# One pool of eight PSUM banks for a hybrid attention layer, scores visited by free banks, two value products joined, and a new order

## The chip, the cores and the metric

The kernel runs on one core of one Trainium2 chip. The time is device microseconds (us) of one execution of the program, and the figure compared is the median of several runs. A profile is one execution taken by the hardware profiler; its span is the time from the first to the last instruction, and the execution's own time is a little longer. TensorE (PE) does matrix products and transposes and writes them to PSUM, which has eight banks of 128 partitions × 512 float32. VectorE (DVE) and ScalarE (ACT) read PSUM and work in SBUF, GpSimd (POOL) works in SBUF, SyncE (SP) issues nearly all transfers (DMAs).

## The reference, cut

One decoder layer, sequence 2048, width 1024, all in float32. A projection makes 4096 columns from the normalised input; 12 heads of 64 attend with three dilated windows, mixed by their softmax denominators; the rest is a gated short convolution; then an output projection, a norm, and the residual.

```python
h = rmsnorm(x, norm_pre_g)
z = jnp.einsum('bsd,de->bse', h, w_in)
q, k, v, g_attn, c_h, c_b, c_c, g_conv = jnp.split(z, cuts, axis=-1)
q = rope(q.reshape(B, S, N_ATTN_HEADS, HEAD_DIM), pos)
k = rope(k.reshape(B, S, N_ATTN_HEADS, HEAD_DIM), pos)
for window, dilation in ((128, 1), (512, 4), (2048, 16)):
    o_i, lse_i = dilated_window_attn(q, k, v, window, dilation)
mix_w = jax.nn.softmax(jnp.stack(lses, axis=0), axis=0)
o = jnp.sum(mix_w[..., None] * jnp.stack(outs, axis=0), axis=0)
attn_out = o.reshape(B, S, ATTN_WIDTH) * jax.nn.silu(g_attn)
conv_out = c_b * causal_depthwise_conv(c_c * c_h, conv_w) * jax.nn.silu(g_conv)
y = jnp.einsum('bse,ed->bsd', jnp.concatenate([attn_out, conv_out], -1), w_out)
x = x + rmsnorm(y, norm_post_g)
```

## The kernel before

The work is cut into 32 units: eight groups of 512 projected columns (group 0 and 7 are the convolution's, 1 to 6 hold one pair of heads each), and for each group four blocks b = 0 to 3 of 512 positions. There are thus 24 attention units. A float32 product is made of three products of fp32r parts (high × high, high × low, low × high), which is why most things come in threes.

**A unit's projection** (from L917): four banks z, each the sum of 8 × 3 matmuls 128x512 (L936 to L938). In an attention unit two banks are made at a time (keys and queries, then values and gate), so a pair of banks takes 48 matmuls; in a convolution unit all four are made together.

**A unit's attention** (attn_unit): ACT and DVE take q and k out of PSUM, rotate them and split them; POOL makes a copy of q in another order for the nearest window (Q1, L646). Then PE makes scores. score4 (L686, matmuls in L694) makes them for the two wider windows, score1 (L711, L722) for the nearest one. Each uses the 64 rows of one head, and the two heads of the pair run side by side on the two halves of the array's rows, into two banks, one per head. A call makes one group: score4 handles 4, 2, 1, 1 of the four residues at b = 0, 1, 2, 3, and score1 two of four blocks, so that a unit has 3, 4, 6, 6 groups. DVE then takes the scores out of PSUM with mask and row minimum (L701, L729), ACT makes exponentials (L705, L733). parts (L740) transposes the probabilities, on PE (L762) with ACT and DVE splitting the result (L767, L768), or on DVE for far blocks (L753 to L755). times (L773) multiplies value tiles with the transposed probabilities: matmuls of 256 columns (L784), the columns being 128 queries, high and low part, into one of two banks O per head. gather (L790) takes O out (L800 to L802).

**The end**: the output projection in seven products per 256 × 1024 block (L1104 to L1106), its norm and the residual.

**What sets the order.** Nothing above is issued at once. Every step is an operation in a plan (add, L166) with an engine, an estimated duration, a priority and the tiles that it reads and writes. schedule (L199) walks through time and gives each engine, whenever it is free, the ready operation of the lowest priority number for which all tiles can be had (_take, L276). Tiles come from rings of slots; a PSUM bank is a slot. The operations are then written out in the order of their planned start, and each engine's queue and the DMA queue are run in that order on the chip. The mode of a PE operation (0 full matmul, 1 scores, 2 transpose) adds to its planned duration when it changes; in modes 1 and 2 the planner first looks for an operation that is also of mode 1 or 2. shift (L190) adds to priorities what the table SHIFT (L117) has for a pair of unit number and place in the code; the table holds what a search found.

PSUM before is parted in two rings: z with 3 banks in a fixed order for projections (L362), st with 5 for all else (L363); convolution units may use 3 + 1 (L364); the output projection uses all eight (L1047). Scores are put into the plan two groups at a time, as one PE operation that needs all four banks:

```python
for i in range(0, len(groups), 2):
    visit = groups[i:i + 2]
    score_last.append(add("PE", sum(g[0] for g in visit), pr, lambda visit=visit: [g[1]() for g in visit], ...
```

Of the kernel before, what the change touches and what calls it, by code (L numbers as in the profile page):

```python
# [28 lines left out]
F32 = mybir.dt.float32  # L29
# [5 lines left out]
DRAM = bass.MemoryType.DRAM  # L35

S, D, C = 2048, 1024, 512
KT = D // 128
NB = S // C
HD = 64  # L40
# [37 lines left out]
class Slot:  # L78
    __slots__ = ("ap", "free")
# [16 lines left out]
class Tok:  # L96


    __slots__ = ("ring", "slot", "left", "end", "hist", "n")
# [9 lines left out]


class Op:
    __slots__ = ("eng", "dur", "prio", "fn", "deps", "toks", "start", "end", "land", "wait", "outs", "ready", "n", "mode", "port", "data")

SHIFT = {  # L117
# [5 lines left out]
}  # L123


class Plan:
# [72 lines left out]
    def schedule(self):  # L199
        engines = ["PE", "ACT", "DVE", "POOL", "DMA"]  # L200
        free = dict.fromkeys(engines, 0.0)
        mode = dict.fromkeys(engines, 0)
        port = bytes_ = 0.0
        cand = {e: [] for e in engines}
        for o in self.ops:
            if not o.wait:
                heapq.heappush(cand[o.eng], (o.prio, o.n, o))
        events = [0.0]
        done = 0
        t = -1.0  # L210
        while done < len(self.ops):
            if not events:
                stuck = sorted((o.prio, o.n, o.eng) for e in engines for _, _, o in cand[e])[:20]
                raise RuntimeError(f"no progress at {t}: {stuck}")
            t2 = heapq.heappop(events)
            if t2 <= t:
                continue
            t = t2
            again = True
            while again:  # L220
                again = False
                for e in engines:
                    if free[e] > t:
                        continue
                    pick = None

                    for kept in ((True, False) if mode[e] else (False,)):
                        skipped = []
                        while cand[e]:
                            item = heapq.heappop(cand[e])  # L230
                            o = item[2]

                            if o.ready <= t and (o.mode or not kept) and not (o.port and port > t) \
                                    and not (o.data and bytes_ > t + 0.5) and self._take(o, t):
                                pick = o
                                break
                            skipped.append(item)
                        for item in skipped:
                            heapq.heappush(cand[e], item)
                        if pick is not None:  # L240
                            break
                    if pick is None:
                        continue
                    o = pick

                    if (o.mode == 1) != (mode[e] == 1):
                        o.dur += 0.2
                    if o.mode == 2 != mode[e]:
                        o.dur += 0.06
                    mode[e] = o.mode  # L250
                    o.start, o.end = t, t + max(o.dur, o.land)
                    if o.data:
                        bytes_ = max(bytes_, t) + o.data
                        o.end = max(o.end, bytes_ + 1.9)
                        heapq.heappush(events, bytes_ - 0.5)
                    free[e] = t + o.dur
                    if o.port:
                        port = free[e]
                    done += 1
                    again = True  # L260
                    heapq.heappush(events, free[e])
                    for k in o.toks:
                        k.left -= 1
                        k.end = max(k.end, o.end + self.lag(e, k.ring.eng))
                        if not k.left:
                            k.slot.free = k.end
                            heapq.heappush(events, k.end)
                    for q in o.outs:
                        q.ready = max(q.ready, o.end + self.lag(e, q.eng))
                        q.wait -= 1  # L270
                        if not q.wait:
                            heapq.heappush(cand[q.eng], (q.prio, q.n, q))
                            heapq.heappush(events, q.ready)
        return t

    def _take(self, op, t):  # L276

# [27 lines left out]


def mmt(n):
    return max(0.109, n * 0.000433 + 0.0071)


def actt(n, psum=False, ptr=False):
# [19 lines left out]
def hybrid_layer(ctx: ExitStack, tc: tile.TileContext, x, w_in, w_out, conv_w, g_pre, g_post,  # L331
                 rope, consts, out):
    nc = tc.nc
    mm = nc.tensor.matmul
# [3 lines left out]
    add = pl.add  # L338
# [4 lines left out]
    cp = ctx.enter_context(tc.tile_pool(name="const", bufs=1))  # L343
    dram = ctx.enter_context(tc.tile_pool(name="dram", bufs=1, space=DRAM))
    psum = ctx.enter_context(tc.tile_pool(name="psum", bufs=1, space=PSUM))

    def ring(pool_, name, n, shape, dt=F32, eng="ACT"):
        return Ring([Slot(pool_.tile(shape, dt, name=f"{name}{i}")) for i in range(n)], name != "st",
                    "PE" if pool_ is psum else eng)

    cst = cp.tile([128, 8 * 128], F32, name="cst")
    ident, perm, mask1, mask4 = cst[:, 0:128], cst[:, 128:256], cst[:, 256:512], cst[:, 512:1024]
    gp = cp.tile([128, KT], F32, name="gp")
    cw = cp.tile([128, 2, 3], F32, name="cw")
    t_d = [dram.tile([128, 3, C], F32, name=f"t{b}") for b in range(NB)]
    xt_d = [[dram.tile([128, 2, C], F32, name=f"xt{b}_{k}") for k in range(KT)] for b in range(NB)]
    mix_d = [dram.tile([KT, 128, C], F32, name=f"mix{b}") for b in range(NB)]
# [1 line left out]
    e_d = [dram.tile([4, 128, 4], F32, name=f"ed{i}") for i in range(2)]  # L359
    a_d = [dram.tile([32, 4, 4, 32], F32, name=f"ad{i}") for i in range(2)]  # L360

    z_r = ring(psum, "z", 3, [128, C])  # L362
    st_r = ring(psum, "st", 5, [128, C])  # L363
    zc_r = Ring(list(z_r) + list(st_r)[:1], False, "PE")  # L364

    xp_r = ring(cp, "xt", 9, [128, 2, C], F32R, "STREAM")
    wp_r = ring(cp, "w", 8, [128, 2, C], F32R)
# [221 lines left out]
    V1, V2 = {}, {}  # L589
    first_attn = []  # L590

    def attn_unit(n, p, b, zs):
# [147 lines left out]
        def parts(h, kind, blk, far=False):  # L740
# [16 lines left out]
            else:  # L757
                ps = Tok(st_r)

                def tr():  # L760
                    for i, (a, c) in enumerate(blk):
                        nc.tensor.transpose(ps.ap[:, i * 128:(i + 1) * 128], pp.ap[:, a, c * 128:(c + 1) * 128], ident)  # L762
                add("PE", 0.111 * m, pr, tr, r=[(pp, a) for a in tiles] + ["cst"], w=[ps, (pt, "hold")], mode=2)

                def p4():
                    return ps.ap[:, :m * 128].rearrange("p (i c) -> p i c", c=128)
# [4 lines left out]


        def times(h, kind, where, O):  # L773
            def pv():
                for (a, c), (pt, i) in sorted(where.items()):
                    dst = O.ap.rearrange("p (l q) -> p l q", l=2)[:, :, (a % 2) * 128:(a % 2 + 1) * 128]
                    if kind == 4:
                        v = V2[p * NB + c].ap[:, a].rearrange("p k d -> p (k d)")[:, h * 128:(h + 1) * 128]
                        s, e = c == 0, c == b
                    else:  # L780
                        t = 4 * b + a - 1 + c
                        v = V1[p * NB + t // 4].ap[:, t % 4, h * 128:(h + 1) * 128]
                        s, e = c == 0 or t == 0, c == 1
                    mm(dst, v, pt.ap[:, i], start=s, stop=e)  # L784
            vs = [V2[p * NB + c] for c in range(b + 1)] if kind == 4 else [V1[p * NB + c] for c in range(max(b - 1, 0), b + 1)]
            attn_last.append(add("PE", mmt(256) * len(where), pr, pv,
                                 r=[(pt, l) for pt in {pt for pt, _ in where.values()} for l in range(2)] + vs, w=[O]))

        UU = {}
# [16 lines left out]
            P[h, 4], P[h, 1] = Tok(p4_r), Tok(p1_r)  # L806

        groups = [score4(r) for r in range(0, 4, per)] + [score1(g) for g in (0, 2)]
        for i in range(0, len(groups), 2):
            visit = groups[i:i + 2]  # L810
            score_last.append(add("PE", sum(g[0] for g in visit), pr, lambda visit=visit: [g[1]() for g in visit], r=[k for g in visit for k in g[2]],
                w=[k for g in visit for k in g[3]], after=x_last, mode=1))
            for g in visit:
                g[4]()

        for kind in (4, 1):
            for h in range(2):
# [97 lines left out]
    for n in range(8 * NB):  # L915
# [12 lines left out]
        for pair in ((range(4),) if conv else (range(2), range(2, 4))):  # L928
          for kt in range(KT):
            for j in pair:  # L930
              xt, w = XT[n, kt], W[grp, kt] if conv else W[grp, j // 2, kt // 2]

              def proj(j=j, kt=kt, xt=xt, w=w, z=zs[j], conv=conv):
# [2 lines left out]
                mm(z.ap, w.ap[:, 0, js], xt.ap[:, 0], start=kt == 0, stop=False)  # L936
                mm(z.ap, w.ap[:, 0, js], xt.ap[:, 1], start=False, stop=False)  # L937
                mm(z.ap, w.ap[:, 1, js], xt.ap[:, 0], start=False, stop=kt == KT - 1)  # L938
              done = add("PE", 3 * (mmt(C) + 0.003), n * 100 + 50 + (kt if conv else j // 2 * 4 + kt / 2), proj, r=[xt, w], w=[zs[j]])
              if n == 0 and kt < 2:  # L940

                later = x_last[2 * kt + 2]
# [101 lines left out]
    tables = [Slot(cs_r[0].ap[:, i]) for i in range(3)]  # L1044
    gated(tables, [o for o in pl.ops if T_last in o.toks], lambda: None)
    xr_r = Ring(tables + list(raw_r))
    oz_r = Ring(list(z_r) + list(st_r), False, "PE")  # L1047
    for q in range(2 * NB):
        b, h = divmod(q, 2)
        po = 3400 + 100 * q  # L1050
# [160 lines left out]
```

## Time and profile before

| what | value |
|---|---|
| median of 3 runs | 1189.88 us (1188.49 to 1190.63) |
| profiled execution | 1189.55 us, its span 1187.8 us |
| score matmuls | L694 and L722, 576 each |
| value products, L784 | 852, mean 284 ns of one, 124.6 us busy |
| transposes of probabilities, L762 | 708, mean 273 ns of one, 98.6 us busy |
| stretch with attention on PE | 139 to 980 us |
| output projection on PE | 1028 to 1181 us |

The mean of one matmul is its time from start to end, and matmuls overlap in the array: a 128x512 row has 0.39 us, while the next starts 0.23 us after it. What PE spends on something is read from differences of starts in the timeline, not from the busy column.

### The profile page before, as it was taken

To read this page: it belongs to the slowest core of one execution; us is meant where nothing else is said; L and a number is where in the kernel's file an instruction comes from. 1 tells how busy PE (TensorE), PEld (TensorE's weight loads), DVE (VectorE), ACT (ScalarE), POOL (GpSimd) and SP (SyncE) were. 2 spreads that over 40 slices of the span, in tenths; PEclk is the share of its full clock that TensorE was granted. 3 is DMA by queue.
4 is the path that set the end of the run, shared out by engine and by line. 5 is a ranking of instruction groups with operands and counts; after the bars stand their busy time and mean duration, and the time that the engine had idled before them with its cause. 6 is when DMAs were issued, how large, how long until landed. Compare 5 with 4: busy or idle time off the path is not lost.

```text
span 1187.8 us, 20832 instructions
## 1 busy us (share of the span) xinstructions
PE 1175.5 (99%) x6716; PEld 981.5 (83%) x6716; DVE 924.7 (78%) x2331; ACT 715.1 (60%) x1875; POOL 266.7 (22%) x212
## 2 busy tenths in 40 slices
PE   9999999999999999999999999999999999999997
PEld 7788888888888888888888888888888888888886
DVE  4665568887788967897688977788788889888886
ACT  6433356765767776775567776576767554454443
POOL 0011123214223232213332222333322122200000
PEclk9999999999999999999999999999999999999999
DMA  9989767877678867687678777788757988645452
GB/s 339 366 340 349 258 227 234 249 246 211 191 212 262 276 198 215 181 289 238 236 229 224 249 201 220 231 262 258 214 162 248 324 260 296 210 145 182 138 186 89
DMA packets 175294, 280.46 MB, mean 236 GB/s; under 512 B 53712, under 2 KB 109776, under 8 KB 175184
## 3 DMA queue, kind: packets, MB, share of 16 engines
q1 hardware_dynamic: 174896, 278.86, 72.6%
q8 instruction: 53, 0.87, 0.3%
q14 instruction: 57, 0.47, 0.1%
q10 hardware_dynamic: 288, 0.27, 0.1%
HBM read 215.42 MB, written 51.05 MB: 224 GB/s over the span
## 4 chain that ended last, share of the span: by engine, by line
PE 92%; DMA 2%; DVE 2%; ACT 2%; issue 1%; SPq 0%; DVEq 0%; ACTq 0%
PE z L936 18%; PE z L938 17%; PE z L937 17%; PE st L784 8%; PE st L762 6%; PE st L694 4%; PE st L722 3%; PE st L1106 3%; PE st L1104 3%; PE st L1105 3%; PE z L1106 2%; PE z L1104 2%; PE z L1105 2%; PE st L936 1%; PE st L938 1%; PE st L937 1%
## 5 line engine op out<-in xcount | busy, mean ns | idle before, releaser
L936 PE MATMUL z<-xt,w 128*128 128x512 f32 x960 | 392.1, 408 | 0.7 <-DVE rp L561 0.5
L938 PE MATMUL z<-xt,w 128*128 128x512 f32 x960 | 375.6, 391 | 0.0
L937 PE MATMUL z<-xt,w 128*128 128x512 f32 x960 | 375.3, 391 | 0.0
L938 PEld LDWEIGHTS z<-xt,w 128*128 128x128 f32 x960 | 180.2, 188 | 39.7
L936 PEld LDWEIGHTS z<-xt,w 128*128 128x128 f32 x960 | 180.7, 188 | 39.1 <-issue 7.9
L937 PEld LDWEIGHTS z<-xt,w 128*128 128x128 f32 x960 | 181.1, 189 | 28.8 <-DVE xt L496 0.3
L705 ACT ACTIVATE p<-p,sm 128x128 f32<-128x128 f32 (+3 forms) x192 | 105.7, 553 | 59.0 <-DVE sm L701 58.9
L768 DVE TENSOR_TENSOR pt<-st,pt 128x512 fp32r<-128x512 f32 (+1 forms) x180 | 116.9, 675 | 24.9 <-ACT pt L767 23.4
L784 PEld LDWEIGHTS st<-pt,v 128*128 128x128 f32 x852 | 117.8, 190 | 12.5 <-DVE pt L768 2.0
L784 PE MATMUL st<-pt,v 128*128 128x256 f32 x852 | 124.6, 284 | 1.1 <-DVE pt L768 1.1
L802 DVE TENSOR_TENSOR uu<-st,uu 64x256 f32<-64x256 f32 x192 | 79.3, 420 | 58.0 <-ACT uu L801 50.4
L767 ACT CAST pt<-st 128x512 fp32r<-128x512 f32 (+1 forms) x180 | 98.3, 579 | 21.5 <-PE st L762 20.4
L800 ACT COPY uu<-st 64x256 f32<-64x256 f32 x192 | 69.5, 367 | 69.1 <-PE st L784 58.2
L701 DVE CUSTOM_DVE_ANT_0 p<-st,cst 128x128 f32<-128x128 f32 (+3 forms) x192 | 81.7, 486 | 31.0 <-PE st L694 30.6
L733 ACT ACTIVATE p<-p,e 128x256 f32<-128x256 f32 (+1 forms) x192 | 94.6, 496 | 18.4 <-DVE e L729 18.3
L844 POOL TENSOR_TENSOR uu<-uu 128x512 f32<-128x512 f32 x48 | 67.7, 1411 | 162.0 <-DVE uu L802 131.5
L762 PE MATMUL st<-cst,p 128*128 128x128 f32 x708 | 98.6, 273 | 0.0
L762 PEld LDWEIGHTS st<-cst,p 128*128 128x128 f32 x708 | 82.4, 141 | 12.5 <-issue 1.0
L801 ACT COPY uu<-st 64x256 f32<-64x256 f32 x192 | 68.8, 367 | 12.1 <-PE st L784 4.7
L729 DVE CUSTOM_DVE_ANT_0 p<-st,cst 128x256 f32<-128x256 f32 (+1 forms) x192 | 67.1, 410 | 9.4 <-PE st L722 9.3
L895 POOL TENSOR_TENSOR uu<-uu 128x512 f32<-128x512 f32 x24 | 36.6, 1527 | 164.9 <-DVE uu L894 164.9
L626 POOL TENSOR_TENSOR rp<-rp,cs 128x512 f32<-128x512 f32 x24 | 35.5, 1480 | 167.9 <-DMA rp<-rp 77.2
(287 smaller groups left out, 1934.1 us busy)
## 6 DMA issues: line engine op xcount, KB each, us to landing
xt<-xt SPq DMA_DIRECT2D x256, 512.0 KB
cs<-t SPq DMA_DIRECT2D x28, 768.0 KB
raw<-in_w_in SPq DMA_DIRECT2D x58, 256.0 KB
rp<-rp SPq DMA_DIRECT2D x192, 64.0 KB
vd<-v SPq DMA_DIRECT2D x24, 512.0 KB
v<-vd SPq DMA_DIRECT2D x96, 128.0 KB
ab<-ad SPq DMA_DIRECT2D x48, 256.0 KB
uu<-mix SPq DMA_DIRECT2D x27, 256.0 KB
```

Of the source, the lines that this page charges most:

```text
L701: add("DVE", dvet(w) + 0.01, pr + URG, lambda h=h, r=r, P4=P4: vec.tensor_tensor_reduce(P4.ap[:, r, 0:w], ps[h].ap[:, (r - r0) * w:(r - r0 ...
L705: add("ACT", actt(w) + 0.19, pr, lambda h=h, r=r, P4=P4: act.activation(P4.ap[:, r, 0:w], P4.ap[:, r, 0:w], AF.Exp, bias=s4(0, h)[:, r:r + ...
L733: add("ACT", actt(256 - lo[g]) + 0.19, pr, lambda h=h, g=g, P1=P1: act.activation(P1.ap[:, g, lo[g]:], P1.ap[:, g, lo[g]:], AF.Exp, bias=E ...
L762: nc.tensor.transpose(ps.ap[:, i * 128:(i + 1) * 128], pp.ap[:, a, c * 128:(c + 1) * 128], ident)
L767: add("ACT", actt(m * 128, True), pr + URG, lambda: act.copy(pt.ap[:, :m, 0, :], p4()), r=[ps], w=[(pt, 0)])
L768: add("DVE", dvet(m * 128), pr + URG, lambda: vec.tensor_tensor(pt.ap[:, :m, 1, :], p4(), f(pt.ap[:, :m, 0, :]), op=ALU.subtract), r=[ps, ...
L784: mm(dst, v, pt.ap[:, i], start=s, stop=e)
L800: add("ACT", actt(256, True) + HALF / 2, pr + URG, lambda: act.copy(cols(a, lo), o()[hi:hi + 64, 0]), r=[O], w=[(a, (h, half))])
L802: add("DVE", dvet(256), pr + URG, lambda: vec.tensor_tensor(cols(a, lo), o()[lo:lo + 64, 0], cols(a, lo), op=ALU.add), r=[O], w=[(a, (h, h ...
L936: mm(z.ap, w.ap[:, 0, js], xt.ap[:, 0], start=kt == 0, stop=False)
L937: mm(z.ap, w.ap[:, 0, js], xt.ap[:, 1], start=False, stop=False)
L938: mm(z.ap, w.ap[:, 1, js], xt.ap[:, 0], start=False, stop=kt == KT - 1)
```

## The change

- **One ring of eight banks.** z and st become one unordered ring that projections, scores, transposes, O and the output projection share.
- **Scores one group at a time.** Each group is a PE operation of its own. The planner begins a visit (goes into mode 1) only when 2 × min(groups left, 2) banks are free; once in mode 1 it may go on with another group if two banks are free. If a score operation has all but its banks, work of lower rank that needs a new bank is passed over in that look (reserved).
- **One product instead of two.** In the nearest window, value tile t serves query block a (as the current block) and a + 1 (as the previous). For a = 0 and 2 their transposed probabilities lie side by side, and one matmul with 512 columns replaces two with 256.
- **Prices in the planner** for PE (matmul, transposes, changes of mode) are changed, and the table SHIFT is another.
- The small tiles gp and cw are laid out ahead of the constants instead of behind them.

```diff
+VISIT = 2
...
 SHIFT = {
-    (-1, 15): 90, (1, 24): -3, (5, 61): 3, (5, 71): 10, (6, 64): 10, (7, 50): 30, (8, 65): -10, (11, 43): 20,
...
+    (-1, 41): 100, (0, 15): 90, (1, 8): 3, (1, 41): 120, (4, 63): 90, (4, 72): 60, (4, 76): 240, (5, 64): 203,
...
-                        skipped = []
+                        skipped, reserved = [], False
                         while cand[e]:
                             item = heapq.heappop(cand[e])
                             o = item[2]

                             if o.ready <= t and (o.mode or not kept) and not (o.port and port > t) \
-                                    and not (o.data and bytes_ > t + 0.5) and self._take(o, t):
-                                pick = o
-                                break
+                                    and not (o.data and bytes_ > t + 0.5):
+                                if reserved and any(k.slot is None and k.ring.eng == "PE" for k in o.toks):
+                                    pass
+                                elif self._enough(o, t, mode[e]) and self._take(o, t):
+                                    pick = o
+                                    break
+                                elif o.mode == 1 and all(k.slot is not None or k.ring.eng == "PE" or self._slot(k, t) for k in o.toks):
+                                    reserved = True
                             skipped.append(item)
...
                     if (o.mode == 1) != (mode[e] == 1):
-                        o.dur += 0.2
+                        o.dur += 0.22
                     if o.mode == 2 != mode[e]:
-                        o.dur += 0.06
+                        o.dur += 0.07
...
+    @staticmethod
+    def _enough(op, t, mode):
+
+        if op.mode != 1 or mode == 1:
+            return True
+        ring = next(k.ring for k in op.toks if k.slot is None and k.ring.eng == "PE")
+        return sum(s.free <= t for s in ring) >= 2 * op.more
...
 def mmt(n):
-    return max(0.109, n * 0.000433 + 0.0071)
+    return max(0.11, n / 2400 + 0.0134)
...
+    gp = cp.tile([128, KT], F32, name="gp")
+    cw = cp.tile([128, 2, 3], F32, name="cw")
     cst = cp.tile([128, 8 * 128], F32, name="cst")
     ident, perm, mask1, mask4 = cst[:, 0:128], cst[:, 128:256], cst[:, 256:512], cst[:, 512:1024]
-    gp = cp.tile([128, KT], F32, name="gp")
-    cw = cp.tile([128, 2, 3], F32, name="cw")
...
-    z_r = ring(psum, "z", 3, [128, C])
-    st_r = ring(psum, "st", 5, [128, C])
-    zc_r = Ring(list(z_r) + list(st_r)[:1], False, "PE")
+    st_r = ring(psum, "st", 8, [128, C])
+    z_r = zc_r = st_r
...
         def times(h, kind, where, O):
+            pairs = [ac for ac in where if kind == 1 and ac[1] == 1 and ac[0] % 2 == 0 and (ac[0] + 1, 0) in where
+                     and where[ac[0] + 1, 0] == (where[ac][0], where[ac][1] + 1)]
+
             def pv():
                 for (a, c), (pt, i) in sorted(where.items()):
                     dst = O.ap.rearrange("p (l q) -> p l q", l=2)[:, :, (a % 2) * 128:(a % 2 + 1) * 128]
+                    if (a - 1, 1) in pairs and c == 0:
+                        continue
+                    if (a, c) in pairs:
+                        t = 4 * b + a
+                        mm(O.ap.rearrange("p (l i q) -> p i l q", l=2, i=2), V1[p * NB + b].ap[:, a, h * 128:(h + 1) * 128],
+                           pt.ap[:, i:i + 2], start=t == 0, stop=False, skip_group_check=True)
+                        continue
...
-        for i in range(0, len(groups), 2):
-            visit = groups[i:i + 2]
-            score_last.append(add("PE", sum(g[0] for g in visit), pr, lambda visit=visit: [g[1]() for g in visit], r=[k for g in visit for k in g[2]],
-                w=[k for g in visit for k in g[3]], after=x_last, mode=1))
-            for g in visit:
-                g[4]()
+        for i, g in enumerate(groups):
+            score_last.append(add("PE", g[0], pr, g[1], r=g[2], w=g[3], after=x_last, mode=1))
+            score_last[-1].more = min(len(groups) - i, VISIT)
+            g[4]()
...
-              done = add("PE", 3 * (mmt(C) + 0.003), n * 100 + 50 + (kt if conv else j // 2 * 4 + kt / 2), proj, r=[xt, w], w=[zs[j]])
+              done = add("PE", 3 * mmt(C), n * 100 + 50 + (kt if conv else j // 2 * 4 + kt / 2), proj, r=[xt, w], w=[zs[j]])
...
-    oz_r = Ring(list(z_r) + list(st_r), False, "PE")
+    oz_r = st_r
```

More of the change, by code (lines that the diff above doesn't have):

```diff
@@ L111 @@
 class Op:
-    __slots__ = ("eng", "dur", "prio", "fn", "deps", "toks", "start", "end", "land", "wait", "outs", "ready", "n", "mode", "port", "data")
+    __slots__ = ("eng", "dur", "prio", "fn", "deps", "toks", "start", "end", "land", "wait", "outs", "ready", "n", "mode", "port", "data", "more")
 SHIFT = {
[5 rows of a table removed]
[9 rows of a table added]
 }
@@ L762, in tr @@
                         nc.tensor.transpose(ps.ap[:, i * 128:(i + 1) * 128], pp.ap[:, a, c * 128:(c + 1) * 128], ident)
-                add("PE", 0.111 * m, pr, tr, r=[(pp, a) for a in tiles] + ["cst"], w=[ps, (pt, "hold")], mode=2)
+                add("PE", 0.109 * m, pr, tr, r=[(pp, a) for a in tiles] + ["cst"], w=[ps, (pt, "hold")], mode=2)
                 def p4():
@@ L783, in pv @@
                         s, e = c == 0 or t == 0, c == 1
-                    mm(dst, v, pt.ap[:, i], start=s, stop=e)
+                    mm(dst, v, pt.ap[:, i], start=s, stop=e, skip_group_check=kind == 1)
             vs = [V2[p * NB + c] for c in range(b + 1)] if kind == 4 else [V1[p * NB + c] for c in range(max(b - 1, 0), b + 1)]
-            attn_last.append(add("PE", mmt(256) * len(where), pr, pv,
+            attn_last.append(add("PE", mmt(256) * (len(where) - 2 * len(pairs)) + mmt(C) * len(pairs), pr, pv,
                                  r=[(pt, l) for pt in {pt for pt, _ in where.values()} for l in range(2)] + vs, w=[O]))
```

12 rows, old and new, of the table SHIFT are left out of this document.

## The prediction

> **What bounds the kernel now.** I read the page first (span, busy shares, the shares of the chain), then the table of stages, then the list of waits of TensorE, and last the timeline of single visits. The page:
>
> ```profile
> span 1187.8 us, 20832 instructions
> PE 1175.5 (99%) x6716; PEld 981.5 (83%) x6716; DVE 924.7 (78%) x2331; ACT 715.1 (60%) x1875; POOL 266.7 (22%) x212
> PE 92%; DMA 2%; DVE 2%; ACT 2%; issue 1%; SPq 0%; DVEq 0%; ACTq 0%
> ```
>
> TensorE (PE) is busy nearly all the time and is 92% of the chain that ended last; DVE, the next engine, is at 78%. The page doesn't say that PE does useful work all the time, only that it rarely waits. How rarely is seen in the table of stages (length, then PE busy) and in the list of what PE waited for (us, times, longest):
>
> ```profile
> 0.00:50.00 50.00, 46.87 (x232) 37.98 (x233) 29.18 (x78) 30.23 (x52) 2.81 (x6) 1.00 0.93 346
> 400.00:500.00 100.00, 99.17 (x623) 83.19 (x622) 79.82 (x220) 67.44 (x195) 31.41 (x26) 1.00 0.73 223
> 500.00:600.00 100.00, 99.71 (x623) 83.46 (x622) 80.23 (x222) 66.11 (x188) 27.04 (x22) 1.00 0.73 237
> 800.00:900.00 100.00, 98.85 (x619) 83.00 (x620) 79.79 (x222) 67.82 (x195) 30.44 (x24) 1.00 0.72 227
> 1080.00:1188.00 108.00, 100.89 (x446) 83.20 (x444) 85.46 (x188) 45.87 (x106) 0.00 (x0) 0.99 0.43 141
> ```
>
> ```profile
> PE st L658 <- DVE rp L618: 1.2, 1, 1.2
> PE st L784 <- DVE pt L768: 1.1, 2, 0.8
> PE z L936 <- DVE rp L561: 0.5, 1, 0.5
> ```
>
> The stages not shown here are full. Idle PE is 50.00 − 46.87 = 3.1 us at the start, 0.83 + 0.29 + 1.15 = 2.3 us in the middle, and 108.00 − 100.89 = 7.1 us at the end (the last tile's normalisation and store). The list puts the stalls of the middle on DVE (L618: 1.2, L768: 1.1), and projections wait 0.5 us once. The granted clock is 1.00 throughout. So there are 2.3 us of waiting to win in the middle and perhaps 1 us at the start; everything else has to come out of PE's own time.
>
> Where PE's own time goes besides useful columns is seen at a visit, that is, a run of score matmuls, which use 64 of 128 rows, two heads side by side. First column: start; the difference of two starts is what PE spent. One visit of 12 and one of 24 score matmuls:
>
> ```profile
> 143.47 0.39 PE L937 MATMUL z<-xt,w 128*128 128x512 f32 x1
> 143.70 0.39 PE L938 MATMUL z<-xt,w 128*128 128x512 f32 x1
> 144.01 1.05 PE L722 MATMUL st<-kk,q 64*128 64x256 f32 x12
> 145.00 0.66 PE L762 MATMUL st<-cst,p 128*128 128x128 f32 x4
> ```
>
> ```profile
> 217.04 0.39 PE L938 MATMUL z<-xt,w 128*128 128x512 f32 x1
> 217.36 1.87 PE L722 MATMUL st<-kk,q 64*128 64x256 f32 x24
> 219.16 0.66 PE L762 MATMUL st<-cst,p 128*128 128x128 f32 x4
> ```
>
> And three visits of one unit with the widest scores:
>
> ```profile
> 515.80 0.39 PE L938 MATMUL z<-xt,w 128*128 128x512 f32 x1
> 516.12 1.67 PE L694 MATMUL st<-kk,q 64*128 64x512 f32 x12
> 517.72 0.50 PE L936 MATMUL z<-xt,w 128*128 128x512 f32 x1
> 518.06 0.39 PE L937 MATMUL z<-xt,w 128*128 128x512 f32 x1
> ...
> 521.32 1.68 PE L694 MATMUL st<-kk,q 64*128 64x512 f32 x12
> ...
> 523.72 0.60 PE L762 MATMUL st<-cst,p 128*128 128x128 f32 x4
> ...
> 527.02 1.87 PE L722 MATMUL st<-kk,q 64*128 64x256 f32 x24
> ```
>
> A projection matmul followed by another takes 143.70 − 143.47 = 0.23 us. The one before a visit takes 0.31 to 0.32, the first one after it 518.06 − 517.72 = 0.34. Each visit costs something for going in and coming out, whatever its length. The three visits stand 5 to 6 us apart.
>
> **Price of one visit.** Two bounds. Lower: two visits of 12 against one of 24, each without the projection's own 0.23, are 2 × (0.08 + 0.99) = 2.14 us against 0.09 + 1.80 = 1.89 us. Both sides do 24 matmuls, so 0.25 us is what the second visit cost by itself. Upper: in the visit at 516.12, 0.09 on entry, 0.11 on the first projection after it, and 1.60 us for six pairs of 512 columns, where six full matmuls take 6 × 0.23 = 1.38: 0.09 + 0.11 + 0.22 = 0.42 us. I take 0.38, nearer to the upper, because the lower leaves out what the leaving costs the work behind a visit (0.11 at a projection).
>
> The Trainium skill, TensorEngine Tiling (Array Packing), Key Properties, says that a change of tiling mode drains the array, and its TensorE: Matmul & The Clock Gate, Phases on the wall clock, gives a drain as about 128 cycles at 2.4 GHz, 53 ns. An estimate from that page is 2 × 0.053 = 0.11 us a visit, and with it the visits' term below would be 1.3 us and the whole forecast 3.3 us later. The trace agrees that a switch costs, and its price is at least twice that, so the trace decides.
>
> **How many visits go.** Before, each unit's groups of scores are joined in twos by hand (L809 to L814). With 1, 2, 4, 4 groups of score4 for b = 0, 1, 2, 3 and two of score1, a unit has 3, 4, 6, 6 groups and 2, 2, 3, 3 visits; with six head pairs that is 60. Each group needs two banks, and the score ring has five, so two groups are all that fit. After, all eight banks are one ring. While a pair of projections accumulates it holds two, which leaves six, three groups. A visit may begin with four free banks and goes on while two more are free and a group is ready. Groups are ready in time: the three visits above have only projections and four transposes between them, so it is banks that part them, and for b = 0 the first visit holds a score1 group already. So a unit's first visit can take three groups. The next can take three more if it is put where six banks are free, or two, with a third visit for the last group, if it starts at four. I count half of the 12 units with six groups at 3 + 3 (6 visits gone), four of the six with three groups at one visit (4 gone), and two of the six with four groups at one (2 gone). That is 12 fewer, 48 left: 12 × 0.38 = **−4.6 us**. Bounds: none gone, 0; and 24 gone (one visit for b = 0 and 1, two for the rest) at 0.42, −10.1 us.
>
> **The joined product.** In L784 two products of the same value tile with 256 columns each become one of 512, twice per head in each unit: 2 × 2 × 24 = 96 pairs, 852 instructions become 756.
>
> ```profile
> 509.12 1.59 PE L784 MATMUL st<-pt,v 128*128 128x256 f32 x12
> 510.56 0.60 PE L762 MATMUL st<-cst,p 128*128 128x128 f32 x4
> ```
>
> Twelve take 510.56 − 509.12 = 1.44 us, 0.120 each, so two cost 0.240. A 512 wide matmul costs 0.227: in a stretch of nothing but projections
>
> ```profile
> 980.50:1028.00 47.50, 47.50 (x211) 39.29 (x211) 41.69 (x66) 17.30 (x32) 10.82 (x7) 1.00 0.78 265
> ```
>
> 47.50 us hold 211 records, of which two are only their neighbours' ends at the edges (a record is 0.39 long): 47.50/209. The gain is 13 ns a pair, 96 × 0.013 = **−1.2 us**. Bounds: −1.3, and, if the output's four pieces of 128 made it slower than a projection, 0.25 instead of 0.227, +1.0. It depends on nothing else: 0.12 us fewer of PE at each place, with its weight load gone too.
>
> **The order and the rest.** The planner's prices for PE change (a projection step of three from 0.695 to 0.680 us, against 3 × 0.227 = 0.68 in the trace; a value product to 0.120, as in the trace; a switch to 0.22 each way, 0.44 a visit, against 0.42 at most above). None of this is an instruction; it changes only the order, and every queue is written in that order anew, SP's and POOL's too. The same DMAs are issued, in other places. What that may do is bounded by PE's waits: the best is that the 2.3 us in the middle go, and the worst I take from a row is three more waits like the largest (1.2 us, DVE late for a transpose), about +4. Prices that now fit the engine speak for few stalls; longer visits make bursts of work for DVE, which was the engine waited for. I take **+1.0 us**. Behind a longer visit on PE wait the transposes and value products of the unit before, and for these ACT and DVE (L767, L768), which have slack of 20 to 30%. The move of the constants' tile behind gp and cw shifts the addresses of identity and masks by the size of these two (56 bytes a partition); two operands of that tile, at different offsets, now cost the same:
>
> ```profile
> L762 PE MATMUL st<-cst,p 128*128 128x128 f32 x708 | 98.6, 273 | 0.0
> L487 PE MATMUL st<-cst,p 128*128 128x128 f32 x96 | 15.1, 275 | 1.3 <-DVE xt L496 1.1 <-DMA p<-in_x 0.2
> ```
>
> so I put it at nothing, with 2 ns × 804 transposes of these two rows = 1.6 us either way as its bound.
>
> **Sum.** −4.6 − 1.2 + 1.0 = −4.8 us on the profiled execution's 1189.55 us (span 1187.8 and 1.75 around it) is 1184.75. That execution lies 0.33 under the median of 1189.88, so the forecast median is **1185.1 us**, 0.4% faster. A measurement here can tell about 0.2% from no change, 2.4 us: under 1187.5 is faster, over 1192.3 slower.
>
> **Rivals.** *Visits hardly fall.* Four free banks let a visit begin, and the drain is slow:
>
> ```profile
> 517.31 0.69 DVE L701 CUSTOM_DVE_ANT_0 p<-st,cst 128x512 f32<-128x512 f32 x1
> 519.15 0.69 DVE L701 CUSTOM_DVE_ANT_0 p<-st,cst 128x512 f32<-128x512 f32 x1
> ```
>
> (first and last of four, one every 0.61 us). The last ends near 519.76 and the next visit starts at 521.32, 1.6 us later. If a visit always starts as soon as the fourth bank is free, the fifth and sixth can be used 1.2 us later at the earliest, and by that row up to 1.6 us more, while two groups of the widest scores take 1.6 us: visits stay at two groups, and only the first of a unit has three, which leaves 3 + 2 + 1 as three visits. Then 1189.9 − 1.2, with a few visits for b = 0, about 1188 us: within 0.2%. The same end comes if the gain is made and stalls take half of it back. For it: the rule asks for four banks, not six. Against: the search can move a visit to where six are free. Chance 0.22.
>
> *Projections starve for banks (the slower side).* A score group that is ready but has too few banks now reserves: later work that needs a new bank is passed over. Before, the projections had three banks of their own, and all their waiting in the list is the 0.5 us of L936. A pair of projections takes 48 × 0.23 = 11 us, then the next needs two new banks. Draining four takes 4 × 0.61 = 2.4 us. If a reservation falls on a pair's start by chance, that is 2.4/11, one in five, with 1.2 us lost on average: 48 × 0.22 × 1.2 = 13 us, and the sum is 1185.1 + 13 = 1198 us. It turns the sign from 7 us of such waits (4.8 + 2.4) on. The Trainium skill, TensorEngine Tiling (Array Packing), PSUM Bottleneck, warns of just this, that faster tiled matmuls don't empty PSUM faster, and the trace agrees: two groups fill four banks in 1.6 us, emptying takes 2.4. For it: DVE at 80% in these stages. Against: the order is fixed ahead by a planner that counts this wait, in prices that the trace bears out, and so can put the visit elsewhere. Chance 0.14.
>
> **How the numbers follow.** The forecast's case has 0.64. With 54 to 36 visits left, and stalls from −2 to +2, its own span is 1178 to 1187.5. Faster by over 0.2%: 0.64. Same: 0.22, the first rival with its eaten-up gain. Slower: 0.14, the second. The range that leaves out no more than 2 in 10 reaches from 1179.5, which leaves out only both gains at their upper bounds with the stalls gone as well, up to 1190.5, which takes in the first rival; beyond it lie most of the slower case and a little of the same.
>
> **What would show it.** Right: fewer runs of L694 and the score1 line between projections, many with 18 matmuls or 36 where they had 12 and 24, the 0.31 to 0.34 us beside each unchanged; the value product's line with 756 instructions, 96 of them 128x512 and 0.227 us from start to start; PE still 99% busy with its instructions down by 96. Wrong: the same 60 runs; a wait of PE's projections (L936) on DVE or ACT that grows from 0.5 us to several; middle stages with PE below 99; a joined product that takes over 0.24 us.

## The result, and the profile after

The changed kernel takes 1181.65 us (median, 1180.81 to 1182.18) against 1189.18 of the kernel before in the same measurement: 7.5 us less, ratio 0.9935, 95% interval 0.9918 to 0.9952. The forecast was 1185.1 (1179.5 to 1190.5), faster.

From the page after, the span and the busy shares:

```profile
span 1179.3 us, 20614 instructions
...
PE 1167.9 (99%) x6620; PEld 980.1 (83%) x6620; DVE 932.6 (79%) x2331; ACT 707.2 (60%) x1875; POOL 268.5 (23%) x212
...
PE 93%; DVE 3%; DMA 2%; ACT 1%; issue 0%; SPq 0%; DVEq 0%; ACTq 0%
```

PE has 96 instructions fewer and is just as full; the other engines have run as many instructions as before. So of the 8.5 us of the span, 1175.5 − 1167.9 = 7.6 came out of PE's busy time and 0.9 out of its idle time, and the shares alone wouldn't have shown it. The unit whose visits the prediction showed, in the timeline of PE after (start, time to the end of the row's last matmul, lines as in the changed file: L711 is score4, L739 score1, L961 to L963 the projection):

```profile
516.42 0.39 PE L963 MATMUL st<-xt,w 128*128 128x512 f32 x1
516.74 2.37 PE L711 MATMUL st<-kk,q 64*128 64x512 f32 x18
519.04 0.50 PE L961 MATMUL st<-xt,w 128*128 128x512 f32 x1
519.38 0.39 PE L962 MATMUL st<-xt,w 128*128 128x512 f32 x1
...
521.64 0.39 PE L963 MATMUL st<-xt,w 128*128 128x512 f32 x1
521.96 0.98 PE L711 MATMUL st<-kk,q 64*128 64x512 f32 x6
522.77 1.79 PE L739 MATMUL st<-kk,q 64*128 64x256 f32 x24
524.50 0.66 PE L779 MATMUL st<-cst,p 128*128 128x128 f32 x4
```

Three groups in the first visit, three in the second, where there had been three visits of two. The steps at the edges are the same as before: 0.32 going in, 0.34 at the first projection behind. Between the L711 and the L739 of the second visit there is no such step, since both use 64 rows. Counted over the whole trace, visits fell from 60 to 43: 11 of the 12 units with six groups have two visits, one of the six with four groups and five of the six with three have a single one.

What PE waited for, after, by the list of waits (total us, times, longest):

```profile
PE st L526 <- DVE sm L435: 1.7, 1, 1.7
PE st L933 <- DVE u L573: 1.1, 1, 1.1
PE st L963 <- DVE w L471: 0.7, 1, 0.7
PE st L811 <- DVE pt L785: 0.2, 1, 0.2
```

The waits of value products and of value transposes on DVE, 1.1 and 1.2 us before, are 0.2 and gone; a wait for the norm's root (L526) at 25 us is new, and L933 is the warm-up's. The table of stages, of after:

```profile
0.00:50.00 50.00, 46.27 (x235) 38.38 (x236) 30.39 (x78) 31.05 (x53) 2.82 (x6) 1.00 0.92 342
400.00:500.00 100.00, 99.30 (x615) 83.83 (x615) 77.71 (x225) 67.14 (x197) 29.97 (x23) 1.00 0.69 219
700.00:800.00 100.00, 99.85 (x607) 83.53 (x606) 88.04 (x234) 72.66 (x209) 27.88 (x24) 1.00 0.70 231
```

Idle PE in the middle fell from 2.3 to 0.7 + 0.15 = 0.85 us, at the start it rose from 3.1 to 3.7. The value products, by form:

```profile
L811 PE MATMUL st<-pt,v 128*128 128x256 f32 x660 | 111.7, 284 | 0.2 <-DVE pt L785 0.2
L801 PE MATMUL st<-pt,v 128*128 128x512 f32 x96 | 38.2, 398 | 0.0
```

96 joined, as forecast.

### The profile page after: what moved, and what is told of

Its sections match the earlier page's. It is cut to its first block, busy times and chain, and to the rows that moved or that the text cites. A ratio compares the mean times of both kernels' runs of the same rounds, so it can differ in the third digit from the quotient of the medians.

```text
span 1179.3 us, 20614 instructions
## 1 busy us (share of the span) xinstructions
PE 1167.9 (99%) x6620; PEld 980.1 (83%) x6620; DVE 932.6 (79%) x2331; ACT 707.2 (60%) x1875; POOL 268.5 (23%) x212
## 4 chain that ended last, share of the span: by engine, by line
PE 93%; DVE 3%; DMA 2%; ACT 1%; issue 0%; SPq 0%; DVEq 0%; ACTq 0%
PE st L961 19%; PE st L963 19%; PE st L962 19%; PE st L779 6%; PE st L811 6%; PE st L1131 4%; PE st L1130 4%; PE st L1129 4%; PE st L711 4%; PE st L739 3%; PE st L801 2%; PE st L504 1%; PE st L675 1%; DMA xt<-xt 1%; DMA g<-in_w_in 0%; DMA p<-in_x 0%
## 5 line engine op out<-in xcount | busy, mean ns | idle before, releaser
L961 PE MATMUL st<-xt,w 128*128 128x512 f32 x1024 | 414.3, 405 | 0.0
L963 PE MATMUL st<-xt,w 128*128 128x512 f32 x1024 | 400.8, 391 | 0.7 <-DVE w L471 0.7
L962 PE MATMUL st<-xt,w 128*128 128x512 f32 x1024 | 399.7, 390 | 0.1
L963 PEld LDWEIGHTS st<-xt,w 128*128 128x128 f32 x1024 | 192.2, 188 | 43.9 <-DVE w L471 1.5
L961 PEld LDWEIGHTS st<-xt,w 128*128 128x128 f32 x1024 | 192.5, 188 | 40.8 <-issue 5.9
L962 PEld LDWEIGHTS st<-xt,w 128*128 128x128 f32 x1024 | 193.0, 188 | 33.1 <-DVE xt L513 0.4
L811 PE MATMUL st<-pt,v 128*128 128x256 f32 x660 | 111.7, 284 | 0.2 <-DVE pt L785 0.2
L811 PEld LDWEIGHTS st<-pt,v 128*128 128x128 f32 x660 | 98.9, 189 | 9.4 <-DVE pt L785 0.9
L869 POOL TENSOR_TENSOR uu<-uu 128x512 f32<-128x512 f32 x48 | 69.5, 1449 | 155.1 <-DVE uu L829 113.4
L779 PE MATMUL st<-cst,p 128*128 128x128 f32 x708 | 95.1, 273 | 0.0
L920 POOL TENSOR_TENSOR uu<-uu 128x512 f32<-128x512 f32 x24 | 37.3, 1556 | 170.1 <-DVE uu L919 170.1
```

The costliest lines, as they stand in the source:

```text
L811: mm(dst, v, pt.ap[:, i], start=s, stop=e, skip_group_check=kind == 1)
```

## The experiments

Two theories at the start. *Visits*: each visit of scores costs PE some 0.38 us for its two switches, 17 are gone, and that is 6.5 of the 7.5 us. *Order*: the new order brought the gain by other ways (fewer waits, fewer runs of transposes, addresses), and switches are cheap. Figures that follow are medians; those of the kernel before beside them were 1189.2 to 1189.6, so a difference under some 0.4 us between two kernels tells nothing.

**Visits put back, nothing else.** After planning, a projection step whose bank and operands are there already is moved into a visit, to stand after its second group. The same matmuls run, in the same order but for these 17.

```diff
     pl.shift()
     hybrid_layer.planned = pl.schedule()
     hybrid_layer.plan = pl
+    hybrid_layer.n_split = pl.split(2, 17)
...
+            z = p.toks[-1]
+            first = not any(q.fn.__name__ == name and z in q.toks for q in pe[:i])
+            if first or any(d.start >= new - 1e-3 for d in p.deps):
+                continue
+            p.start = new
```

> The changed kernel with its planned order, except that 17 projection steps (three matmuls each, whose bank and operands are there already) are issued inside a visit instead of behind it, so that there are 60 visits of scores again instead of 43. No matmul more or fewer. Visit theory (a visit costs 0.38 us): 17 x 0.38 = 6.5 us slower than the changed kernel's 1181.65, about 1188.1. Rival (the new order gained by other things, and a switch costs no more than two drains of 0.053 us): 17 x 0.11 = 1.8 us, about 1183.5.

1188.06 us. The first visit that was split, in this kernel's timeline (L737 is score4, L987 to L989 the projection):

```profile
207.37 0.39 PE L989 MATMUL st<-xt,w 128*128 128x512 f32 x1
207.69 1.34 PE L737 MATMUL st<-kk,q 64*128 64x384 f32 x12
208.95 0.50 PE L987 MATMUL st<-xt,w 128*128 128x512 f32 x1
209.29 0.39 PE L988 MATMUL st<-xt,w 128*128 128x512 f32 x1
209.51 0.39 PE L989 MATMUL st<-xt,w 128*128 128x512 f32 x1
209.83 0.80 PE L737 MATMUL st<-kk,q 64*128 64x384 f32 x6
210.56 0.51 PE L987 MATMUL st<-xt,w 128*128 128x512 f32 x1
210.91 0.39 PE L988 MATMUL st<-xt,w 128*128 128x512 f32 x1
```

and the same place in the changed kernel, whole:

```profile
206.99 0.39 PE L963 MATMUL st<-xt,w 128*128 128x512 f32 x1
207.30 1.87 PE L711 MATMUL st<-kk,q 64*128 64x384 f32 x18
209.10 0.50 PE L961 MATMUL st<-xt,w 128*128 128x512 f32 x1
209.44 0.39 PE L962 MATMUL st<-xt,w 128*128 128x512 f32 x1
```

From the projection ahead to the second one behind, 210.91 − 207.37 = 3.54 us against 209.44 − 206.99 = 2.45. The split visit holds three projection matmuls more, 3 × 0.227 = 0.68, and 0.41 is the price of the visit. Over all 17: (1188.06 − 1181.65)/17 = 0.38 us by the medians, (1186.1 − 1179.3)/17 = 0.40 by the spans. No stalls came with it: all that PE waited for in this kernel's list adds up to 4.0 us, and to 4.5 in that of after. With 60 visits the kernel is back within 0.1% of the one before: ratio 0.9993, 0.9983 to 1.0002.

**Twice as many.** The same with 59 steps moved, pl.split(1, 999), that is, behind every group where such a step was to be had.

> The same with 59 projection steps issued inside visits, 99 visits instead of 43. Visit theory: 56 x 0.38 = 21 us, about 1203. If the price is the lower bound of 0.25: 14 us, about 1196. Rival of two drains: 56 x 0.11 = 6 us, about 1188. Stalls of DVE or ACT that the shifted steps bring would show as idle PE in the stages and are to be taken off.

1204.81 us, (1204.81 − 1181.65)/56 = 0.41 us a visit, 0.42 by the spans (1203.1 and 1179.3). The list of waits of this kernel is as short as that of after (4.2 us in all), so it is price, not stalls; its longest:

```profile
PE st L552 <- DVE sm L461: 1.7, 1, 1.7
PE st L959 <- DVE u L599: 1.1, 1, 1.1
PE st L989 <- DVE w L497: 0.8, 2, 0.6
PE st L837 <- DVE pt L811: 0.4, 2, 0.2
```

43, 60 and 99 visits lie nearly on one line; the price is settled at 0.38 to 0.41 us by the medians.

**Runs of transposes put back.** The new order also has 129 runs of transposes where there were 159. Here 30 projection steps are moved in between transposes, pl.split(1, 30, (2,)).

> The changed kernel, with 30 projection steps issued between the transposes of a run of transposes: 159 runs of transposes as before instead of 129, and 43 visits. If the fewer runs of transposes had a part in the gain, at the planner's 0.07 us each, 30 x 0.07 = 2.1 us slower, about 1183.8. By the trace of before a run of four transposes between projections takes 0.90 us from the projection ahead to the second one behind, against 2 x 0.227 + 4 x 0.109 = 0.89, so 30 x 0.01 = 0.3 us, about 1182, which is no difference.

1181.89 us, 0.24 more, within the spread of either kernel. That part of the order theory falls: a transpose between full matmuls costs next to nothing besides itself.

**Products unjoined.** In the changed order, each joined product is issued as two again (planned times kept):

```diff
-                    if (a - 1, 1) in pairs and c == 0:
-                        continue
-                    if (a, c) in pairs:
+                    if False:
```

> The changed kernel in its own order, with the 96 joined value products issued as 192 products of 256 columns again. Forecast's price: 96 x 0.013 = 1.2 us slower, about 1182.9, and PE's time for value products 852 x 0.120 = 102.2 us instead of 660 x 0.120 + 96 x 0.227 = 101.0. If the joined form costs 0.235 as its starts in the changed kernel's trace suggest, 0.5 us.

1182.19 us, 0.54 more, at the lower of the two expectations; a difference as small as this is near what the runs can tell. The trace says the same: in the changed kernel the time from a joined product's start to the next start is 0.235 us in the mean of 96, not the projections' 0.227, and 2 × 0.120 − 0.235 = 0.005, 0.5 us for all. The output's four pieces are not the reason: a projection matmul right behind a product of 256 columns takes 0.235 too (mean of 81 in the changed kernel), and the 15 joined products right behind a full matmul have a median of 0.227. It is the place behind a shorter product that the price of 0.227, taken from a stretch of projections alone, left out.

**What the search did, and what the banks did.** Four kernels with an empty SHIFT table, so that the planner's rules alone make the order: the kernel before; the changed one with PSUM parted 3 + 5 as before; with eight banks and groups joined by hand in twos; and the changed one with nothing else altered.

```diff
-SHIFT = {
-    (-1, 41): 100, (0, 15): 90, (1, 8): 3, (1, 41): 120, (4, 63): 90, (4, 72): 60, (4, 76): 240, (5, 64): 203,
...
+SHIFT = {}
```

> The kernel before with an empty SHIFT table, so that the order is what the planner's rules give without a search: 60 visits in its order. The base for the next three. Both theories: slower than 1189 by what the search had given, some 3 to 10 us, all of it idle PE and longer waits, none of it visits.

> The changed kernel with an empty SHIFT table and the old parting of PSUM, 3 banks for projections and 5 for the rest: groups one at a time, joined product, new prices. 60 visits in its order, since five banks hold two groups. Visit theory: as the base without a search, less 0.5 us for the joined product and whatever the new prices bring. Rival (it is the rule of single groups that gains, whatever the banks): some us faster than that base.

> The changed kernel with an empty SHIFT table, eight banks in one ring, but the groups joined in twos by hand as before: 55 visits in its order. Visit theory: against the parted PSUM (60 visits) 5 x 0.4 = 2 us faster. Rival (more banks for projections take stalls away, visits matter little): the larger part of the gain is here already, and the next one adds nothing.

> The changed kernel with an empty SHIFT table alone: eight banks, groups one at a time, 47 visits in its order. Visit theory: against twos by hand (55) 8 x 0.4 = 3.2 us faster, against the parted PSUM (60) 13 x 0.4 = 5.2 us, and against the changed kernel slower by 4 x 0.4 = 1.6 us of visits plus the stalls that the search takes away. If the search had made the gain, it is no faster than the kernel before without its search, less 0.5 us.

They took 1193.12, 1203.60, 1193.45 and 1191.67 us, with 60, 60, 55 and 47 visits. The last is only 1.45 us faster than the first, and their runs overlap (1190.18 to 1195.69 and 1192.27 to 1196.16), although 13 visits fewer are worth 13 × 0.4 = 5.2. To see where the rest went I added up, over the starts of all PE instructions, what each step took beyond the usual one of its kind and place (0.227 for a full matmul, 0.32 going into a visit, 0.345 coming out, 0.120 for a value product, and so on), leaving out what is under 0.03 us: 10.4, 21.5, 13.0 and 14.0 us of waiting in the four, 7.3 in the kernel before and 6.3 in the changed one. From the first to the last, −5.2 for visits, −0.5 for joined products and +3.6 of waiting are −2.1 us, against −1.45 measured and −0.8 by the spans (1190.5 and 1189.7). From twos by hand to single groups, −3.2 for visits and +1.0 of waiting are −2.2, against −1.8 measured. From the kernel without the search to the changed kernel, 4 × 0.4 for visits and 14.0 − 6.3 for waiting are 9.3 us, against 10.0 measured.

My two expectations for the parted PSUM were wrong. It takes 10.5 us more than the kernel before without its search, where 0.5 less was expected, and the changed kernel without a search gains 11.9 us on it, not 5.2. Most of this, 10.15 us, is there with eight banks and twos by hand: 8.5 of waiting and 5 × 0.4 of visits, 10.5 by that count. So the rival named for that kernel, that more banks take stalls away, was right in this pair. Why parted banks are so slow here is open: this kernel has single groups, the reservation and the new prices as well, and none of these was taken out alone. Its list of waits shows value products (L802) and transposes (L792) behind DVE:

```profile
PE st L802 <- DVE pt L776: 6.8, 6, 1.5
PE st L792 <- DVE pt L776: 3.4, 4, 0.8
PE z L1122 <- DVE xt L1089: 2.1, 1, 2.1
```

and in the changed kernel without a search the longest new wait is in the output projection, which the search had cleared:

```profile
1044.56 0.39 PE L1119 MATMUL st<-w,xt 128*128 128x512 f32 x1
1046.66 0.50 PE L1120 MATMUL st<-w,xt 128*128 128x512 f32 x1 [1.71 <-DVE ys L1139]
```

So the pool and the rule for visits take away 13 of the 17 visits with no search at all; the search takes four more, and above all the waits that the rules leave. In time, the rules alone gain nothing that is clear of the spread: 1191.67 us is 2.3 more than the kernel before takes with its own search. The new table is longer than the old one (60 entries for 34), and a search as long for the kernel before was not run. That kernel has 60 visits with its search and without, so what a longer one could win there is waiting, 7.3 us by this count, of which the changed kernel keeps 6.3. The planner's new prices were not taken out alone either, so their part in the order is open.

**Six free banks asked for.** VISIT = 3, empty SHIFT.

> As the changed kernel with an empty SHIFT table (47 visits, 1191.67), but a visit may begin only with six free banks (or two per group left): 44 visits in its order. Visit theory alone: 3 x 0.4 = 1.2 us faster, about 1190.5. The forecast's slower rival, projections that starve while a group reserves banks, is made as strong as it can be here: then PE idles ahead of scores and projections, and the time is 10 us or more longer, over 1200, with stages well below full.

1196.22 us, 4.6 slower than with two, with 44 visits. The sign is the starving theory's, the size is under half of the 10 us that it said. Waiting, added up as above, is 21.6 us instead of 14.0, so +7.6 − 3 × 0.4 = 6.4, against 6.3 by the spans (1196.0 and 1189.7). The list names mostly waits for data (value products and the output projection behind DVE, a projection behind a DMA), so that projections starve for banks isn't shown by it:

```profile
PE st L801 <- DVE pt L775: 2.7, 4, 1.4
PE st L1121 <- DVE xt L1088: 2.3, 1, 2.3
PE st L951 <- DMA xt<-xt: 1.0, 2, 0.7
```

**No reservation.** In the same kernel, reserved stays False.

> As the changed kernel with an empty SHIFT table (47 visits, 1191.67), without the reservation: later work may take a bank while a score group waits. 50 visits in its order. Visit theory: 3 x 0.4 = 1.2 us slower, about 1192.9. If the reservation itself starved projections at four banks, its removal makes the kernel faster than 1191.

1193.90 us, 2.2 slower than with it, 50 visits: 3 × 0.4 and 0.3 of waiting (14.3 against 14.0) are 1.5. In this order the reservation at four banks doesn't starve the projections, and it saves three visits.

**The constants' place.** The changed kernel with the constants' tile ahead of gp and cw again.

> The changed kernel with the constants' tile ahead of gp and cw again, as before. Forecast: nothing, 1181.65 within 1 us. Rival: identity and masks at another address change the pace of transposes (708 + 96) or of DVE's takeover of the scores, by 1 to 2 us.

1181.42 us, no difference.

## Why the prediction was right in sign and short in size

- *PE's own time is the bound, and switches are in it:* right, and shown by the visits put back.
- *0.38 us a visit:* right, 0.38 to 0.41 by two kernels that changed nothing but the place of projection steps. The lower bound of 0.25, from two visits with transposes behind them, was too low, and an estimate of two drains of 53 ns from the Trainium skill (TensorE: Matmul & The Clock Gate, Phases on the wall clock) is about a quarter of it.
- *48 visits left, −4.6 us:* the term that was mis-sized. 43 are left, 17 × 0.38 = 6.5 us (17 × 0.40 = 6.8 of the span). I counted half of the units with six groups at 3 + 3; it was 11 of 12. Five of six with three groups, not four, have one visit, one of six with four groups, not two. Without any search the rules leave 47 visits, close to the 48, with 8 of the 12 at 3 + 3; the search took the other four. The worry behind the half, that a visit starts at the fourth bank and so takes two groups, was worked from how banks came free in the trace of before, where other work had been put into that time; no run shows that this is why it was too strong.
- *Joined products, −1.2 us:* mis-sized. 0.5 us, because a joined product stands mostly behind one of 256 columns and there takes 0.235 us to the next start, as a projection matmul does in that place, not the 0.227 of a stretch of projections. It lies within the bounds given.
- *Order and the rest, +1.0 us:* wrong in sign. Waiting fell: 2.3 to 0.85 us idle in the middle, 3.1 to 3.7 at the start, together 0.85 less. The runs show that this was the search's work; without it waiting is 14.0 us, and the kernel takes 1191.67 us, so that the gain on the searched kernel before is gone.
- *The rivals:* visits that hardly fall did not come, not even without a search (13 fewer). Projections that starve for banks did not come either with four banks asked for (without the reservation the kernel is slower); asking for six costs 4.6 us where the order isn't searched, with waits that are mostly for data. I had put the waits down to a meeting by chance, 13 us, and named the planner's foresight as the reason against it; the short lists of waits fit that, but no run took the foresight away alone.
- *The sum:* −6.5 − 0.5 − 0.85 = −7.85, against −7.5 of the medians and −8.5 of the spans. The forecast's terms missed by −1.9, +0.7 and −1.85. The two larger misses go the same way, so the sign owes nothing to errors that cancel; that more waiting was forecast and less came is the search's doing, as the kernels without it show.

## What to carry to other kernels

On an engine that is 99% busy, look at the differences of starts at the places where the kind of work changes; what is paid there is counted as busy, and here 60 changes were 24 us. Put a price on one change from the starts at all its edges (0.42 us here); the difference of two runs of unlike length gave only 0.25, because it left out what is paid behind them. Then count how many the buffers allow, by letting the planner's rule run over the units rather than by the buffers' state in the old order. A test that puts the changes back and leaves all else settles such a price to a few hundredths of a us; a comparison of two orders, each without its search, can't do that, since waits of the same size come and go with the order.

## What the runs showed of the hardware

A visit of half-height matmuls (64 of the 128 rows) between full ones costs 0.38 to 0.41 us beyond its columns. The starts of the single matmuls in the visit at 516.74 of the changed kernel show four parts: 0.09 at the matmul ahead, 0.11 at the first pair, 0.09 at the last pair and 0.11 at the first full matmul behind. A run of transposes between full matmuls costs next to nothing (30 runs more, 0.24 us). Going from one kind of half-height matmul to another inside a visit costs nothing that the rows show. A matmul with 512 columns takes 0.235 us to the next start right behind a product of 256 columns, whether its output is one piece (mean of 81) or four pieces of 128 (mean of 80), and 0.227 in a stretch of its own kind. Moving the constants by 56 bytes a partition changed nothing (1181.42 and 1181.65 us).
